# Row sums of a 64 MB array: from "112 rows and 16 behind" in one part to "127 rows and one behind" in four parts

## The chip, the core and the metric

The kernel runs on one core of a Trainium2 chip. A core has five instruction streams, of which three matter here: VectorE (DVE in the profile), ScalarE (ACT) and SyncE (SP), which does no arithmetic and issues DMA transfers. Sixteen DMA engines move data between the device memory (DRAM) and SBUF, the on-chip memory of 128 partitions. The metric is the device time of one launch in microseconds (us). Before the change it is 161.98 us, the median of three runs (161.95 to 162.12).

## The reference

```
batch, seq, dim = 32, 512, 1024          # x: float32, 64 MiB; multiplier = 0.5
out = (np.sum(x, axis=-1) * multiplier).astype(np.float32)
```

Seen flat, x has 16384 rows of 1024 floats (4 KB each), and every row becomes one number of `out`. Each byte of x is read once and used once: 67.11 MB go in and 65.5 KB come out.

## The kernel before

The 16384 rows are dealt to the 128 partitions, 128 rows each. Partition p owns 112 consecutive rows (`x_rows`), and, behind all of these, 16 further consecutive rows in the last 2048 rows of x (`x_last`). The output is cut the same way (`out_rows`, `out_last`). So every partition has 128 results, columns 0 to 127 of the SBUF tile `res`: columns 0 to 111 for its 112 rows, columns 112 to 127 for the last 16.

The work runs over eight blocks of 16 rows for each partition (8 MiB a block). The first seven are one load each (line 98), in which every partition gets one run of 64 KB. They go into a pool of three buffers, `x_pool`, so load b + 3 waits for the work on block b. The last block comes in five loads: 8, 5 and 2 rows (line 117), and then the last row in two pieces, of 544 and 480 floats (line 123), into the tile `end`. That is the sequence of blocks 16, 8, 5, 2, 1. SP issues all loads, in this order, on one queue, and the first three are moved ahead of the program's entry by `start_loads_at_entry`.

Six of the first seven blocks are summed by DVE with one instruction each (line 100, 16 rows), which is followed by a small scaling instruction (line 103). The seventh block is shared, half to DVE and eight rows to ACT (`act_row`, line 74). The last block's rows are shared row by row: ACT takes rows 4 to 7, 11, 12 and 14, and DVE the others with `dve_sum` (line 84), a fused add of two halves with an accumulator. The last row of each partition is summed by two such instructions, one for each piece: the first leaves its sum in `end` beside the second piece, and the second adds it in and writes column 127 of `res`.

There are two stores, both issued by SP. The early one (line 127) writes columns 0 to 111 when the first seven blocks are done, and stands in the queue behind the last loads. The last one (line 145) writes columns 112 to 127, 64 bytes for each partition, and waits for the last DVE instruction. In front of it stands an instruction that does nothing but wait for the loads and for ACT (`seen`, made by `nop_after`, line 63), so that these waits are over by then. Behind it another such instruction waits for the early store and the last DVE instruction; the program's end waits for the last store.

Of the kernel before, what the change touches and what calls it, by code (L numbers as in the profile page):

```python
# [1 line left out]

# [4 lines left out]


@with_exitstack
def kernel(  # L10
    ctx: ExitStack,
    tc: tile.TileContext,
    x: bass.AP,
    multiplier: float,
    out: bass.AP,
):

    nc = tc.nc
    P = nc.NUM_PARTITIONS
    fp32 = mybir.dt.float32  # L30
    ADD = mybir.AluOpType.add

    x_flat = x.flatten_outer_dims()
    N, D = x_flat.shape
    rows = N // P
    out_flat = out.rearrange("b s -> (b s)")
    mul = float(multiplier)

    B = 16
    n_blocks = rows // B  # L40
    assert N == P * rows and rows == n_blocks * B
    own = rows - B
    x_rows = x_flat[0 : P * own, :].rearrange("(p c) d -> p c d", p=P)
    x_last = x_flat[P * own : N, :].rearrange("(p c) d -> p c d", p=P)
    out_rows = out_flat[0 : P * own].rearrange("(p c) -> p c", p=P)
    out_last = out_flat[P * own : N].rearrange("(p c) -> p c", p=P)

    x_pool = ctx.enter_context(tc.tile_pool(name="x", bufs=3))
    res_pool = ctx.enter_context(tc.tile_pool(name="res", bufs=1))
    sums = res_pool.tile([P, rows], fp32, name="sums")  # L50
    res = res_pool.tile([P, rows], fp32, name="res")
    cut = 544
    at = 576
    end = res_pool.tile([P, at + D - cut], fp32, name="end")
    nc.vector.memset(end[:, at - 2 : at], 0.0)  # L55

    SYNC = mybir.DependencyInfo(mybir.DependencyClass.Sync, mybir.DependencyReason.DATA)
    ORDER = mybir.DependencyInfo(
        mybir.DependencyClass.NoSync, mybir.DependencyReason.SCHED_ONLY
    )  # L60

    def nop_after(engine, waits_for, follows):
        i = engine.nop()
        for w in waits_for:
            tc.add_manual_dep(i.ins, w.ins.name, SYNC, reason="end seen here")
        for f in follows:
            tc.add_manual_dep(i.ins, f.ins.name, ORDER, reason="in this order")
        return i

    loads = []  # L70
    acts = []

    def act_row(t, r, col):
        acts.append(nc.scalar.activation(  # L74
            out=t[:, r, :],
            in_=t[:, r, :],
            func=mybir.ActivationFunctionType.Copy,
            scale=mul,
            accum_out=res[:, col : col + 1],
        ))  # L80

    def dve_sum(row, dst, scale):
        mid = row.shape[-1] // 2
        return nc.vector.tensor_tensor_reduce(  # L84
            out=row[:, 0:mid],
            in0=row[:, 0:mid],
            in1=row[:, mid:],
            scale=scale,
            scalar=0.0,
            op0=ADD,  # L90
            op1=ADD,
            accum_out=dst,
        )

    for b in range(n_blocks - 1):
        c0 = b * B
        t = x_pool.tile([P, B, D], fp32, name="xb")
        loads.append(nc.sync.dma_start(out=t, in_=x_rows[:, c0 : c0 + B, :]))  # L98
        h = B if b < n_blocks - 2 else B // 2
        nc.vector.reduce_sum(  # L100
            out=sums[:, c0 : c0 + h], in_=t[:, 0:h, :], axis=mybir.AxisListType.X
        )
        nc.vector.tensor_single_scalar(  # L103
            out=res[:, c0 : c0 + h],
            in_=sums[:, c0 : c0 + h],
            scalar=mul,
            op=mybir.AluOpType.mult,
        )
        for r in range(h, B):
            act_row(t, r, c0 + r)  # L110

    c0 = (n_blocks - 1) * B
    t = x_pool.tile([P, B, D], fp32, name="xb")
    pieces = [(0, 8), (8, 13), (13, 15)]
    for lo, hi in pieces:
        loads.append(
            nc.sync.dma_start(  # L117
                out=t[:, lo:hi, :], in_=x_last[:, lo:hi, :]
            )
        )  # L120
    for to, lo, hi in ((0, 0, cut), (at, cut, D)):
        loads.append(
            nc.sync.dma_start(  # L123
                out=end[:, to : to + hi - lo], in_=x_last[:, B - 1, lo:hi]
            )
        )
    early = nc.sync.dma_start(out=out_rows, in_=res[:, 0:own])
    on_act = {4, 5, 6, 7, 11, 12, 14}
    for r in range(B - 1):
        if r in on_act:  # L130
            act_row(t, r, c0 + r)
        else:
            dve_sum(t[:, r, :], res[:, c0 + r : c0 + r + 1], mul)
    first = dve_sum(end[:, 0:cut], end[:, at - 1 : at], 1.0)
    part_seen = nop_after(nc.vector, [first], [])
    final = dve_sum(end[:, at - 2 :], res[:, rows - 1 : rows], mul)

    tc.add_manual_dep(final.ins, part_seen.ins.name, ORDER, reason="in this order")
    tc.declare_no_dep(final.ins, first.ins.name, reason="waited for by the nop in front")

    seen = nop_after(nc.sync, loads[-8:] + acts[-1:], [])
    store = nc.sync.dma_start(out=out_last, in_=res[:, own:])
    tc.add_manual_dep(store.ins, seen.ins.name, ORDER, reason="in this order")
    for a in acts[-len(on_act) :]:
        tc.declare_no_dep(store.ins, a.ins.name, reason="waited for by the nop in front")
    nop_after(nc.sync, [early, final], [store])

    def start_loads_at_entry(nc_):

        entry, *rest = nc_.main_func.blocks
        is_sp = lambda i: i.engine == mybir.EngineType.SP
        is_load = lambda i: type(i).__name__ == "InstDMACopy"
        for block in rest:
            body = list(block.instructions)
            own = [i for i in body if is_sp(i)]  # L160
            if not any(is_load(i) for i in own):
                continue
            lead = []
            for i in own:
                if not is_load(i) or i.sync_info.on_wait:
                    break
                lead.append(i)
            names = {i.name for i in lead}
            block.instructions = [i for i in body if i.name not in names]
            head = list(entry.instructions)  # L170
            at = next(
                k for k, i in enumerate(head) if is_sp(i) and type(i).__name__ == "InstDrain"
            )
            entry.instructions = head[:at] + lead + head[at:]
            return

    nc.at_finalize(start_loads_at_entry)


# [1 line left out]
_INS = ['x', 'multiplier']  # L181
_OUTS = [((32, 512), 'float32')]

_NUMBERS = {'multiplier': 0.5}


# [26 lines left out]
```

## Time and profile before

| what | value |
|---|---|
| median of three runs | 161.98 us (161.95 to 162.12) |
| profiled execution: span from first to last instruction | 160.2 us |
| median less that span (what lies around it) | 1.78 us |
| DVE busy | 119.3 us (74%), 35 instructions |
| ACT busy | 17.3 us (11%), 31 instructions |
| moved by DMA | 67.18 MB, 419 GB/s on average over the span |
| share of the 16 DMA engines' time in use | 97.6% |

The profile gives only the span of the profiled execution; its time outside is not recorded, so 1.78 us is taken from the median. "DMA share" is the mean busy share of the 16 DMA engines, and "us to landing" is the time from the start of a DMA's issue to the moment at which all of its data has arrived. "SPq" is SP issuing, as against computing.

### The profile page before, as it was taken

What the parts mean: (1) busy time and instruction counts of PE and PEld (TensorE: products, weight loads), DVE (VectorE), ACT (ScalarE), POOL (GpSimd) and SP (SyncE); (2) the same over time, 40 slices, a digit from 0 to 9 for tenths busy, and PEclk for the clock granted to TensorE, in tenths of its full rate; (3) what the DMA queues carried; (4) which work ended last, traced back from release to release, by engine and by line L of the source; (5) the groups of instructions that cost most, each with busy time, mean ns of one, the idle gap of its engine ahead of it and who ended that gap; (6) DMA issues with size and microseconds to landing.
All of it is one profiled execution on the core that took longest, in us unless ns stands there. A gap on an engine that the chain in (4) does not pass through costs nothing.

```text
span 160.2 us, 139 instructions
## 1 busy us (share of the span) xinstructions
DVE 119.3 (74%) x35; ACT 17.3 (11%) x31; POOL 0.2 (0%) x4
## 2 busy tenths in 40 slices
DVE  0000059998799968999599995999959999597543
ACT  0000000000000000000000000000000000599952
POOL 0000000000000000000000000000000000000000
DMA  8996996996996997997998989979969969999992
GB/s 278 507 524 262 524 524 262 524 524 262 524 507 278 524 475 311 524 442 344 524 425 360 524 360 425 524 327 458 524 295 491 524 278 507 393 401 422 424 395 76
DMA packets 2016, 67.18 MB, mean 419 GB/s; under 512 B 480, under 2 KB 608, under 8 KB 736
## 3 DMA queue, kind: packets, MB, share of 16 engines
q1 hardware_dynamic: 2016, 67.18, 97.6%
HBM read 67.11 MB, written 0.07 MB: 419 GB/s over the span
## 4 chain that ended last, share of the span: by engine, by line
DMA 75%; DVE 22%; SPq 1%; issue 0%; DVEq 0%
DMA xb<-in_x_dram 51%; DMA end<-in_x_dram 24%; DVE sums L100 22%; SPq L117 1%; SPq L123 0%; DVE end L84 0%; SPq L98 0%; DVE res L103 0%; DVEq L208 0%
## 5 line engine op out<-in xcount | busy, mean ns | idle before, releaser
L100 DVE TENSOR_REDUCE sums<-xb 128x16 f32<-128x16384 f32 (+1 forms) x7 | 112.0, 16002 | 31.5 <-DMA xb<-in_x_dram 31.5
L74 ACT ACT_TABLE_LOAD x1 | 1.3, 1283 | 138.0 <-DMA xb<-in_x_dram 138.0
L74 ACT ACTIVATE xb<-xb 128x1024 f32<-128x1024 f32 x15 | 15.7, 1044 | 2.1 <-DMA xb<-in_x_dram 2.1
L84 DVE CUSTOM_DVE_ANT_0 xb<-xb 128x512 f32<-128x512 f32 x8 | 5.1, 690 | 4.9 <-DMA xb<-in_x_dram 4.9
L74 ACT ACTIVATION_READ_ACCUMULATOR xb<-xb 128x1 f32 x15 | 2.8, 187 | 0.0
L55 DVE MEMSET end<- 128x2 f32 x1 | 0.1, 60 | 1.8 <-PEq L194 1.8
L103 DVE TENSOR_SCALAR res<-sums 128x16 f32<-128x16 f32 (+1 forms) x7 | 1.2, 174 | 0.2
L84 DVE CUSTOM_DVE_ANT_0 end<-end 128x272 f32<-128x272 f32 (+1 forms) x2 | 0.9, 426 | 0.2 <-DMA end<-in_x_dram 0.2
L84 DVE DVE_READ_ACCUMULATOR2_ANT res<- 128x1 f32 x9 | 0.7, 83 | 0.0
L194 POOL MEMSET const-bfloat16-1.0<- 128x1 bf16 x1 | 0.1, 102 | 0.0
L194 POOL MEMSET const-uint8-127<- 128x1 uint8 x1 | 0.1, 102 | 0.0
L194 POOL MEMSET const-float32-0.0<- 128x1 f32 x1 | 0.1, 99 | 0.2 <-issue 0.2
L194 POOL MEMSET const-float32-1.0<- 128x1 f32 x1 | 0.1, 99 | 0.0
L84 DVE DVE_READ_ACCUMULATOR2_ANT end<- 128x1 f32 x1 | 0.1, 83 | 0.0
## 6 DMA issues: line engine op xcount, KB each, us to landing
xb<-in_x_dram SPq DMA_DIRECT2D x1, 4096.0 KB, 31.1
xb<-in_x_dram SPq DMA_DIRECT2D x1, 2560.0 KB, 36.9
xb<-in_x_dram SPq DMA_DIRECT2D x1, 1024.0 KB, 38.9
end<-in_x_dram SPq DMA_DIRECT2D x1, 272.0 KB, 39.0
end<-in_x_dram SPq DMA_DIRECT2D x1, 240.0 KB, 39.2
xb<-in_x_dram SPq DMA_DIRECT2D x7, 40.8
out_dram<-res SPq DMA_DIRECT2D x1, 56.0 KB, 10.0
out_dram<-res SPq DMA_DIRECT2D x1, 8.0 KB, 1.4
```

What stands on the lines that cost most here:

```text
L55: nc.vector.memset(end[:, at - 2 : at], 0.0)
L74: acts.append(nc.scalar.activation(out=t[:, r, :], in_=t[:, r, :], func=mybir.ActivationFunctionType.Copy, scale=mul, accum_out=res[:, col ...
L84: return nc.vector.tensor_tensor_reduce(out=row[:, 0:mid], in0=row[:, 0:mid], in1=row[:, mid:], scale=scale, scalar=0.0, op0=ADD, op1=ADD, ...
L100: nc.vector.reduce_sum(out=sums[:, c0 : c0 + h], in_=t[:, 0:h, :], axis=mybir.AxisListType.X)
L103: nc.vector.tensor_single_scalar(out=res[:, c0 : c0 + h], in_=sums[:, c0 : c0 + h], scalar=mul, op=mybir.AluOpType.mult,)
L117: nc.sync.dma_start(out=t[:, lo:hi, :], in_=x_last[:, lo:hi, :])
L194: nc = _bacc.Bacc("TRN2", target_bir_lowering=False, num_devices=1)
```

## The change

Rows are dealt in another way, and there are three stores in place of two.

- x is seen as four parts of 4096 rows. Partition p = 4g + b (g from 0 to 31, b from 0 to 3) owns, in part b, the 127 rows from row 127g on, and one single row from the part's last 32 rows, row 4064 + g. `x_rows`, `x_single`, `out_rows` and `out_single` say this, with the DRAM side in three dimensions: 32 (g), 4 (b), and a run.
- The loads have the same sizes and order as before. Blocks 0 to 6 and the pieces of 8, 5 and 2 rows are now from the 127 consecutive rows. The last row, in two pieces, is the single one.
- The early store still writes columns 0 to 111, now as 128 runs of 448 bytes that begin 508 bytes apart in each part; before, these runs joined to one contiguous range.
- A new store, `second`, is issued by ACT behind its last row. It writes columns 112 to 126: 128 runs of 60 bytes.
- The last store, on SP, writes column 127 alone: 4 bytes for each partition, which in `out` form four contiguous runs of 128 bytes, one at the end of each part.
- The waiting instruction at the end waits for `second` too.

```diff
+    G = P // 4
+    long = rows - 1
+    x_regions = x_flat.rearrange("(b n) d -> b n d", b=4)
+    out_regions = out_flat.rearrange("(b n) -> b n", b=4)
+    x_rows = x_regions[:, 0 : G * long, :].rearrange("b (g c) d -> g b c d", c=long)
+    x_single = x_regions[:, G * long :, :].rearrange("b g d -> g b d")
+    out_rows = out_regions[:, 0 : G * long].rearrange("b (g c) -> g b c", c=long)
+    out_single = out_regions[:, G * long :].rearrange("b (g o) -> g b o", o=1)
...
-        loads.append(nc.sync.dma_start(out=t, in_=x_rows[:, c0 : c0 + B, :]))
+        loads.append(nc.sync.dma_start(out=t, in_=x_rows[:, :, c0 : c0 + B, :]))
...
-                out=t[:, lo:hi, :], in_=x_last[:, lo:hi, :]
+                out=t[:, lo:hi, :], in_=x_rows[:, :, own + lo : own + hi, :]
...
-                out=end[:, to : to + hi - lo], in_=x_last[:, B - 1, lo:hi]
+                out=end[:, to : to + hi - lo], in_=x_single[:, :, lo:hi]
...
-    early = nc.sync.dma_start(out=out_rows, in_=res[:, 0:own])
+    early = nc.sync.dma_start(out=out_rows[:, :, 0:own], in_=res[:, 0:own])
...
+    second = nc.scalar.dma_start(out=out_rows[:, :, own:], in_=res[:, own:long])
     seen = nop_after(nc.sync, loads[-8:] + acts[-1:], [])
-    store = nc.sync.dma_start(out=out_last, in_=res[:, own:])
+    store = nc.sync.dma_start(out=out_single, in_=res[:, long:])
...
-    nop_after(nc.sync, [early, final], [store])
+    nop_after(nc.sync, [early, second, final], [store])
```

More of the change, by code (lines that the diff above doesn't have):

```diff
@@ L42 @@
     own = rows - B
[L43 to L46, printed above, removed]
+    G = P // 4
[6 more added lines that the diff above has]
+    out_single = out_regions[:, G * long :].rearrange("b (g o) -> g b o", o=1)
     x_pool = ctx.enter_context(tc.tile_pool(name="x", bufs=3))
```

## The prediction

> **What bounds the kernel now.** I read the chain that ended last first, to see what the end hangs on. Its columns are start, length and what.
>
> ```profile
> 99.28 17.23 DVE sums L100
> 116.52 0.02 issue
> 116.54 0.19 DVE res L103
> ...
> 117.91 0.43 SPq L123
> 118.34 0.04 issue
> 118.38 39.17 DMA end<-in_x_dram
> 157.55 0.02 issue
> 157.58 0.41 DVE end L84
> ```
>
> The chain alternates between loads and DVE's sums only because a load's issue waits for a free buffer. The last step shows the truth: the last load was issued at 118.38 and landed 39.17 us later, because it stood behind what was already queued. So the second view is the busy table by stretches: length, busy time of DVE, ACT and POOL, clock, DMA share, GB/s.
>
> ```profile
> 5.00:22.00 17.00, 0.09 (x1) 0.00 (x0) 0.00 (x0) 1.00 1.00 432
> 41.20:60.60 19.40, 17.41 (x3) 0.00 (x0) 0.00 (x0) 1.00 1.00 432
> ...
> 138.00:147.70 9.70, 8.85 (x3) 9.64 (x17) 0.00 (x0) 1.00 0.99 425
> ...
> 153.80:156.30 2.50, 1.94 (x7) 2.20 (x5) 0.00 (x0) 1.00 0.98 399
> 156.30:157.60 1.30, 1.14 (x5) 1.14 (x2) 0.00 (x0) 1.00 0.56 197
> 157.60:160.20 2.60, 0.39 (x2) 0.00 (x0) 0.00 (x0) 1.00 0.04 3
> ```
>
> All sixteen DMA engines are busy all the time from 5 us on, at 432 GB/s, and DVE needs 17.4 us of each 19.4 us block. The packet records agree: one 64 KB run takes 2.418 us on its engine, 27.1 GB/s, and 16 x 27.1 = 434 GB/s. The load stream is the bound until 157.1, when the last engine is through; the first is through at 156.6. What comes behind it is a fixed tail, shown by the timeline (start, length) and the list of DMA issues (KB, us to landing).
>
> ```profile
> 157.58 0.41 DVE L84 CUSTOM_DVE_ANT_0 end<-end 128x241 f32<-128x241 f32 x1 [0.16 <-DMA end<-in_x_dram]
> 157.91 0.08 DVE L84 DVE_READ_ACCUMULATOR2_ANT res<- 128x1 f32 x1
> 158.02 0.34 SPq L145 DMA_DIRECT2D out_dram<-res  x1
> ```
>
> ```profile
> out_dram<-res SPq DMA_DIRECT2D x1, 56.0 KB, 10.0
> out_dram<-res SPq DMA_DIRECT2D x1, 8.0 KB, 1.4
> ```
>
> The last store is issued at 158.02 and has landed at 159.45 (1.43 us by the records); 0.75 us of closing barriers make 160.20. The early store (56 KB) was issued at 147.79 and landed 10.0 us later, at 157.79: it waits in the queue behind the loads. The sum below is made against this execution: span 160.20, and 1.78 us around it to the median of 161.98.
>
> **The change, part by part.**
>
> *Loads: the same bytes, sizes, order and number.* Only the DRAM addresses move. A partition's runs began 112 rows (448 KB) apart; now four neighbouring partitions read 16 MB apart, and every fourth is 127 rows (508 KB) further. Runs stay contiguous, 64 KB in the seven large blocks. Since an engine is at 2.418 us for such a run through the whole stream, there is nothing to gain there. The one slow place is the start: the first run of each engine took 3.07 to 3.47 us (one 2.77), about 0.8 us over 2.418. I read that as the first access's latency and take 0; lower bound -0.8. Upwards the trace shows no other address pattern, so there is no row: 1% of the stream's 156 us would cost 1.6 us, and a pattern that halved the rate 156 us. I take 0, because the reads stay long contiguous runs like those of the rows above, and the last pieces, only 2 KB long and 64 KB apart, still went at 24.7 GB/s on an engine (88 ns for 2176 bytes), so this stream has borne a change of steps before.
>
> The Trainium skill, "DMA: Bandwidth & Descriptors", section "Latency and other measured facts", has a rule against this: partition rows a large power of two apart slow DMA copies to less than half (103 against 214 GB/s at 4 and 8 MiB), and a pad of 4 KiB mends it. By it the loads would cost up to some 160 us more, an estimate, if streams 16 MiB apart ran side by side; 508 KiB, being 512 less 4, is on its good side. No run here shows it yet.
>
> *Issue of the loads, with a three-dimensional DRAM side.* Issues took 0.38 us (the first) to 0.46 us. Eleven of the twelve lie beside queued transfers (39 us deep at the end); if that cover were gone they would cost their 0.4 us each. The first is exposed. Bounds 0 and +0.08 (0.46 - 0.38); I take +0.05.
>
> *DVE and ACT sums:* the same instructions in the same order, 0.
>
> *Early store:* 448-byte runs 508 bytes apart instead of joined. It used to land at 157.79, and nothing that mattered waited for it. Now something does: in the changed program ACT's new store carries a wait for the early store's landing, since their ranges of `out` interleave. I keep 157.79; the bound is that its runs take twice as long (they ran from 156.42 to 157.28 by the records), so landing up to 0.9 us later.
>
> *Second store, on ACT.* It waits for DVE's last row but the single one (column 125, written by 156.99), for ACT's own last row (column 126, 157.44), and for the early store, 157.79, which is the last. Issue 157.85, and with SP's 1.43 us to landing it is in at 159.28, beside the last store's 159.45: hidden by 0.17 us. Nothing is queued behind it on ACT but the end barrier. If the early store or the issue on ACT takes over 0.17 us more, it sets the end. ACT issues no DMA in the trace of before. Bounds from SP's rows: nothing, to a full landing behind the store, +1.43. I take +0.10, for two issues that overlap from 158.02 to 158.20 and for twice the small writes landing together (their runs occupy 0.2 us, 158.86 to 159.07, per store).
>
> *Last store: 128 runs of 4 bytes instead of 64.* The number of runs stays, and that governs: a 64-byte run takes 8 to 11 ns, a 4-byte completion record 9 ns. So the bytes save nothing; at best the 0.2 us in which the runs pass (-0.2). Against it, 32 pieces from different engines now fall into one 128-byte range. Each run's completion came 0.36 to 0.39 us after it; if an engine's eight pieces went strictly one after the other, that is 8 x 0.36 = 2.9 us, the upper bound. I take +0.15, near the lower end, since the other small stores landed at the common pace. Its issue has three dimensions: 0.34 us up to 0.46; I take +0.05. The wait for ACT's rows goes from its conditions, but it had long been over (157.44), so 0.
>
> *Closing:* one wait more on SP, before the landing of the last store. It is hidden while `second` lands first; otherwise two waits of some 0.06 us follow it. I take +0.05.
>
> Sum: 0.05 + 0.10 + 0.15 + 0.05 + 0.05 = +0.40. The span becomes 160.6, the time 162.4 us. A measurement of this kernel can tell about 0.2% (0.32 us) from no change, so this is slower by a little.
>
> **The rivals.**
>
> *The tail stays hidden (no change), 162.0.* For it: `second` has 0.17 us of cover, a store of fewer bytes may land as early, issues differ by less than 0.1. Then every term is near zero: 161.7 to 162.3. Against it: the new wait for the early store leaves little room.
>
> *The start gets faster (faster), 161.5.* One mechanism: the 0.8 us that the first runs of the engines took too long is due to the addresses, and the new ones avoid most of it; the whole stream and with it the tail move forward. It decides once it saves over 0.7 us with the tail's +0.4, or over 0.32 us with a tail at 0. Price: -0.4 to -0.8, 161.2 to 161.6. Against it: a slow first access is what any stream that starts cold would show, and later 64 KB runs show no trace of address trouble.
>
> *The load stream gets slower, 163 to over 300.* The sixteen engines run at an even 27.1 GB/s each, which holds only while neither DRAM nor the split of 128 partitions over engines makes two engines meet. The change touches both: the DRAM side has 32 as its outer dimension, the SBUF side 128. It shows from 0.2% of the rate on (+0.3); 1% gives 163.6, half the rate some 318 us. Against it: the number of engines and the runs are unchanged.
>
> **How the numbers follow.** Tail longer, as summed: 0.40 (162.3 to 163.4). No change: 0.25. Start faster: 0.17. Stream slower: 0.18, of which 0.08 below 164 and 0.10 beyond. So faster 0.17, same 0.25, slower 0.58. The range leaves out the stream's large losses (0.10) and the lowest part of the faster case: 161.5 to 164.0, which holds the no-change case and most of the price of `second` (+1.43). The likeliest case's own range is 162.3 to 163.4.
>
> **What would show it.** In the changed profile: 64 KB loads still 19.4 us apart and a DMA share of 1.00 near 432 GB/s (else the stream rival); the first DVE sum still at 21.9 (earlier: the start rival); the last DVE instruction near 157.6; a DMA issue on ACT near 157.85 and one on SP near 158.02; landings of 1.4 to 1.6 us for both, and SP's last wait for out_dram a few tenths over 1.0 us. If ACT's issue comes clearly later than 157.9, or its landing ends last by more than half a microsecond, the second store was undersized. Anything over 164 means the stream was misjudged, and the tail's account is then of no weight.

## The result and the profile after

The changed kernel takes 169.79 us (median of four runs, 169.61 to 170.41) against 162.0 us before. The ratio is 1.0489, with a 95% interval of 1.0471 to 1.0508: slower by 7.8 us. The profiled execution took 169.61 us, of which 167.8 us are its span; 1.8 us lie around it as before.

The load stream is as it was. In the busy table by stretches (length, DVE, ACT, POOL, clock, DMA share, GB/s) of the changed kernel:

```profile
5.00:22.00 17.00, 0.00 (x0) 0.00 (x0) 0.00 (x0) 1.00 1.00 432
...
41.20:60.60 19.40, 17.39 (x2) 0.00 (x0) 0.00 (x0) 1.00 1.01 436
...
157.00:163.00 6.00, 1.55 (x6) 1.36 (x4) 0.00 (x0) 1.00 0.12 31
163.00:165.00 2.00, 0.00 (x0) 0.00 (x0) 0.00 (x0) 1.00 0.00 0
165.00:168.00 3.00, 0.00 (x0) 0.00 (x0) 0.00 (x0) 1.00 0.00 0
```

The engines still move 432 to 436 GB/s without a gap. The time is lost at the two ends. First the start, in the chain that ended last (start, length, what):

```profile
0.00 0.66 SPq L102
0.66 0.05 issue
0.70 41.73 DMA xb<-in_x_dram
42.44 0.02 issue
42.46 17.23 DVE sums L104
```

Before the change the same chain had:

```profile
0.00 0.38 SPq L98
...
41.23 17.23 DVE sums L100
```

The first issue takes 0.66 us instead of 0.38, and DVE's second sum begins at 42.46 instead of 41.23, 1.23 us later. This shift stays to the end of the loads: DVE's last sum begins at 158.84 instead of 157.58, 1.26 us later. Now the tail, in the timeline (start, length), the list of DMA issues (KB, us to landing) and the waits of SP (us, times, longest):

```profile
158.84 0.41 DVE L88 CUSTOM_DVE_ANT_0 end<-end 128x241 f32<-128x241 f32 x1 [0.19 <-DMA end<-in_x_dram]
159.16 0.63 ACTq L148 DMA_DIRECT2D out_dram<-res  x1
159.18 0.08 DVE L88 DVE_READ_ACCUMULATOR2_ANT res<- 128x1 f32 x1
159.29 0.57 SPq L150 DMA_DIRECT2D out_dram<-res  x1
```

```profile
out_dram<-res SPq DMA_DIRECT2D x1, 56.0 KB, 10.0
out_dram<-res ACTq DMA_DIRECT2D x1, 7.5 KB, 1.9
out_dram<-res SPq DMA_DIRECT2D x1, 0.5 KB, 7.8
```

```profile
SPq L213 <- DMA out_dram<-res: 6.0, 1, 6.0
```

Before the change this last wait of SP was:

```profile
SPq L208 <- DMA out_dram<-res: 1.0, 1, 1.0
```

The last store now moves 0.5 KB instead of 8 KB and needs 7.79 us from its issue to landing instead of 1.43, so 6.36 us more. The records of single pieces show that all 128 pieces had left the engines at 160.92; the sixteen engines' completions then trickle in from 161.92 to 167.07, where before they came within 0.17 us. With 1.26 us from the start this is 7.62 us, and the spans differ by 7.6.

So two questions had to be settled by experiments: what makes the last store land so late, and what delays the start. For the store there were three theories. Crowding: pieces that fall close together in DRAM hold one another up. Size: any 4-byte write is slow. Neighbours: the pieces collide with those of the other two stores. For the start there were two: the third dimension of the loads, or their new addresses.

### The profile page after: what moved, and what is told of

It reads as the page before. It is cut to its first block, busy times and chain, and to the rows that moved or that the text cites. A ratio compares the mean times of both kernels' runs of the same rounds, so it can differ in the third digit from the quotient of the medians.

```text
span 167.8 us, 141 instructions
## 1 busy us (share of the span) xinstructions
DVE 119.3 (71%) x35; ACT 17.3 (10%) x31; POOL 0.2 (0%) x4
## 4 chain that ended last, share of the span: by engine, by line
DMA 72%; DVE 21%; SPq 2%; issue 0%; DVEq 0%
DMA xb<-in_x_dram 49%; DMA end<-in_x_dram 23%; DVE sums L104 21%; SPq L121 1%; SPq L102 0%; SPq L127 0%; DVE end L88 0%; DVE res L107 0%; DVEq L213 0%
```

## The experiments

### One part instead of four

The changed kernel with 127 rows and one behind in a single part. The DRAM sides have two dimensions again; column 127 is 512 contiguous bytes, still written in 4-byte pieces.

```diff
-    x_rows = x_regions[:, 0 : G * long, :].rearrange("b (g c) d -> g b c d", c=long)
-    x_single = x_regions[:, G * long :, :].rearrange("b g d -> g b d")
+    x_rows = x_flat[0 : P * long, :].rearrange("(p c) d -> p c d", c=long)
+    x_single = x_flat[P * long :, :]
...
-    out_single = out_regions[:, G * long :].rearrange("b (g o) -> g b o", o=1)
+    out_single = out_flat[P * long :].rearrange("(p o) -> p o", o=1)
...
```

> The changed kernel in one part instead of four: 128 partitions own 127 consecutive rows and one of the last 128 rows, so the DRAM side of every transfer has two dimensions again, and the last column is 512 contiguous bytes of out, written in 4-byte pieces. The theory for the 1.2 us at the start (a third dimension makes issue and hand-out to the DMA engines slower): first load lands at 21.9 us as before the change, issues 0.38 to 0.46 us. Its rival (the new addresses are slower to read at first): 508 KB steps remain, so up to 1.2 us may remain if these are the cause, nothing if the 16 MB steps are. For the 6.4 us at the end, the theory of crowding (4-byte writes into the same few DRAM lines are done one after another) and that of size (any 4-byte write to DRAM is slow) both expect a landing of 6 to 8 us after the issue, so about 168.4 us in all; the theory of neighbours (writes beside the other two stores collide) expects the same or less.

Measured: 167.82 us, ratio 1.0355 (1.0339 to 1.0371). The chain's beginning and the list of DMA issues:

```profile
0.00 0.37 SPq L100
0.37 0.05 issue
0.42 40.80 DMA xb<-in_x_dram
```

```profile
out_dram<-res ACTq DMA_DIRECT2D x1, 7.5 KB, 1.5
out_dram<-res SPq DMA_DIRECT2D x1, 0.5 KB, 7.0
```

The start of this execution is the old one (issue 0.37 us, first load at 21.91). That steps of 127 rows cost nothing in two dimensions is not shown by it: the seven further kernels below with the same large loads had their first load at 21.96 to 22.31, and the one profile of the kernel before at 21.89, so a few tenths of a microsecond may be theirs. The late landing stays, at 7.0 us. Third dimension and four parts are not its cause.

### Four parts, with 16 rows behind

The kernel before in four parts, its last store of 64 bytes for each partition kept.

```diff
-    x_rows = x_flat[0 : P * own, :].rearrange("(p c) d -> p c d", p=P)
-    x_last = x_flat[P * own : N, :].rearrange("(p c) d -> p c d", p=P)
...
+    x_rows = x_regions[:, 0 : G * own, :].rearrange("b (g c) d -> g b c d", c=own)
+    x_last = x_regions[:, G * own :, :].rearrange("b (g c) d -> g b c d", c=B)
...
```

> The kernel before, in four parts: in each, 32 partitions own 112 consecutive rows and 16 behind them; two stores, the last of 64 bytes for each partition. Three-dimensional theory for the start: first load lands 1.2 us later than before the change, at 23.1, and the last store's issue takes 0.57 us instead of 0.34. Crowding and size both expect the last landing back at about 1.4 + 0.4 us, so 161.98 + 1.2 + 0.4 = 163.6 us in all. If the tail were the fault of three dimensions, it would stay near 169.

Measured: 163.14 us, ratio 1.007 (1.0055 to 1.0085). The first load lands at 22.55, less late than expected, and the last store 1.81 us after its issue. Four parts with their third dimension, in loads and stores, cost about 1.2 us, and the rest of the 7.8 us goes with the one-column store.

### The third dimension alone

The kernel before; only the seven large loads get a third dimension, at nearly the old addresses.

```diff
-    x_rows = x_flat[0 : P * own, :].rearrange("(p c) d -> p c d", p=P)
+    G = P // 4
+    x_groups = x_flat[0 : G * (4 * own + 1), :].rearrange("(g r) d -> g r d", g=G)
+    x_rows = x_groups[:, 0 : 4 * own, :].rearrange("g (b c) d -> g b c d", c=own)
...
```

> The kernel before, whose seven large loads alone get a third dimension on the DRAM side: groups of four partitions, each group moved by one row against the last, so addresses move by at most 31 rows (the sums are of these rows, so part of the output belongs to rows displaced by up to 31). Stores and last block as before. If three dimensions make the start slow: first load lands at 23.1, all else as before, 163.2 us. If the addresses 16 MB apart do: lands at 21.9, 162.0 us.

Measured: 162.57 us, ratio 1.0036 (1.0022 to 1.005), between the two expectations. The beginning of its chain:

```profile
0.00 0.63 SPq L100
0.63 0.06 issue
0.69 41.05 DMA xb<-in_x_dram
```

The issue takes 0.63 us with a third dimension at nearly the old addresses, and the first load lands at 22.42, 0.53 us late. The piece records show how: the first engine begins at 1.42 instead of 1.01, and the last of the sixteen at 2.24 instead of 1.51. This is not one execution's chance: over all profiles of this case the last engine begins between 1.35 and 2.05 in the ten kernels with two-dimensional large loads, and between 2.13 and 2.52 in the eight with three. So half of the 1.2 us is explained. The other half was still open.

### The last store alone, as in the change

The changed kernel without its other two stores.

```diff
-    early = nc.sync.dma_start(out=out_rows[:, :, 0:own], in_=res[:, 0:own])
...
-    second = nc.scalar.dma_start(out=out_rows[:, :, own:], in_=res[:, own:long])
...
-    nop_after(nc.sync, [early, second, final], [store])
+    nop_after(nc.sync, [final], [store])
```

> The changed kernel without its early and second stores: only column 127 is written, the rest of out is left out. Crowding and size: the last store still lands 7.8 us after its issue, 169.5 us in all. Neighbours: 1.9 us after its issue, some 163.6 us in all.

Measured: 169.08 us in one run, landing 7.0 us after the issue:

```profile
out_dram<-res SPq DMA_DIRECT2D x1, 0.5 KB, 7.0
```

The theory of neighbours falls: the store lands late with no other store in the program. (The 0.8 us between 7.79 and 7.0 are one execution each, and stay open.)

### The pieces' distance

Crowding and size were still to be told apart. In the one-part kernel, with the last store alone, the 4-byte pieces were put 4, 8, 16, 64 and 512 bytes apart, from the start of `out` on. (At 4 bytes this changes only the place in `out`, and the landing stays: 7.14 us against the one-part kernel's 6.99.) The edit, for 16 bytes:

```diff
-    out_single = out_flat[P * long :].rearrange("(p o) -> p o", o=1)
+    step = 4
+    out_single = out_flat[0 : P * step].rearrange("(p o) -> p o", o=step)[:, 0:1]
```

> The one-part kernel with 127 rows and one behind, without its early and second stores: the only store writes 4 bytes for each partition, at the start of out, 4 bytes apart (512 contiguous bytes; the rest of out is left out). Crowding and size both expect what the one-part kernel showed: landing 7.0 us after the issue, some 167.8 us in all.

> As the store alone at 4 bytes apart, but 16 bytes apart, so that a quarter as many writes share any stretch of out (only these numbers are written). Crowding: the part of the landing over 1.4 us falls from 5.6 to about a quarter, landing 2.5 to 3.5 us. Size: 7 us still.

> As the store alone, 64 bytes apart (only these numbers are written). Crowding with a stretch of 64 bytes: landing 1.4 to 1.6 us, 162.0 us in all; with a larger stretch, more. Size: 7 us still.

> As the store alone, 512 bytes apart (only these numbers are written). Crowding: landing 1.4 to 1.6 us, 162.0 us in all. Size: 7 us still, 167.6 us in all.

> The store alone of the one-part kernel, 8 bytes apart (only these numbers are written). At 16 bytes it landed in 1.44 us, at 4 bytes in 7.1 us. If writes collide when they share 16 bytes: two do so now, and the landing lies between, some 3 us or more. If they collide only where they share 8 bytes or adjoin: 1.44 us.

Measured, one run each:

| pieces of 4 bytes, bytes apart | pieces in 16 bytes | landing after issue | device time |
|---|---|---|---|
| 4 | 4 | 7.14 us | 168.01 us |
| 8 | 2 | 2.94 us | 163.88 us |
| 16 | 1 | 1.44 us | 162.63 us |
| 64 | 1 | 1.45 us | 162.29 us |
| 512 | 1 | 1.44 us | 162.28 us |

The lists of DMA issues at 4, 8 and 16 bytes, in this order:

```profile
out_dram<-res SPq DMA_DIRECT2D x1, 0.5 KB, 7.1
```

```profile
out_dram<-res SPq DMA_DIRECT2D x1, 0.5 KB, 2.9
```

```profile
out_dram<-res SPq DMA_DIRECT2D x1, 0.5 KB, 1.4
```

The same 128 pieces of 4 bytes, 512 bytes in all, land in 1.44 us or in 7.14 us: size is not the cause, closeness is. My expectation for 16 bytes (2.5 to 3.5 us) missed. The loss doesn't fall in proportion to the distance; it ends sharply between 8 and 16 bytes. (The kernel at 16 bytes is 0.3 us slower than those at 64 and 512 with the same landing: its first load landed 0.14 to 0.16 us later than theirs, at 22.31, and the last load 0.36 to 0.37 us later. That part of the time is the load stream's.)

### The pieces' width

If what counts is that two pieces share 16 bytes, adjoining pieces of 8 bytes must collide and adjoining ones of 16 bytes must not. The last two, or four, columns were stored alone, side by side.

```diff
-    step = 1
-    out_single = out_flat[0 : P * step].rearrange("(p o) -> p o", o=step)[:, 0:1]
+    wide = 4
+    out_single = out_flat[0 : P * wide].rearrange("(p o) -> p o", o=wide)
...
-    store = nc.sync.dma_start(out=out_single, in_=res[:, long:])
+    store = nc.sync.dma_start(out=out_single, in_=res[:, rows - wide :])
```

> The store alone of the one-part kernel, but of the last two columns, 8 adjoining bytes for each partition, 1 KB in all (the rest of out is left out). Stretch of 16 bytes shared by two pieces: as with 4 bytes at steps of 8, about 2.9 us to landing. If the size of a piece, 4 bytes, is what hurts when neighbours are near: 1.4 us.

> The store alone of the one-part kernel, of the last four columns, 16 adjoining bytes for each partition, 2 KB in all (the rest of out is left out). Stretch of 16 bytes: no piece shares one, 1.4 us to landing. A larger stretch, or any adjoining pieces: over 2 us.

The lists of DMA issues, of 8 and of 16 bytes:

```profile
out_dram<-res SPq DMA_DIRECT2D x1, 1.0 KB, 2.7
```

```profile
out_dram<-res SPq DMA_DIRECT2D x1, 2.0 KB, 1.4
```

Landing 2.68 us and 1.45 us; 163.62 and 162.10 us. Two pieces of 8 bytes in one stretch of 16 collide about as two of 4 bytes do, and pieces of 16 bytes side by side don't. So what these runs show is a stretch of 16 bytes that several pieces share. Every one of these stores began at the start of `out`; whether the stretches lie at multiples of 16 bytes or any two pieces less than 16 bytes apart collide was not tried.

### Where the rest of the start comes from

The kernel before, stores and last block unchanged, its large loads in three dimensions from three more sets of addresses. The edit for the changed kernel's own addresses:

```diff
-    x_rows = x_flat[0 : P * own, :].rearrange("(p c) d -> p c d", p=P)
+    G = P // 4
+    x_regions = x_flat.rearrange("(b n) d -> b n d", b=4)
+    x_rows = x_regions[:, 0 : G * 127, :].rearrange("b (g c) d -> g b c d", c=127)
...
```

> The kernel before, stores and last block unchanged, with only the seven large loads taken from the addresses of the changed kernel (four parts, runs 127 rows apart, of which the first 112 rows are used, so the sums belong to other rows). If the 1.2 us at the start of the changed kernel come from its loads alone: first load lands at 23.1, 163.2 us. If half of it came from the rest of the program: 22.4 to 22.5 and 162.6 us.

> The kernel before, stores and last block unchanged, the seven large loads in three dimensions but with neighbouring partitions 127 rows apart in one stretch (groups of four, moved by one row each; sums of displaced rows). If the 0.6 us beyond the cost of the third dimension come from the step of 127 rows: first load at 23.1, 163.2 us; if from the 16 MB between the parts: 22.4, 162.6 us.

> As the one with four parts and 127 rows, but runs 112 rows apart (sums of displaced rows). If the 0.6 us come from the 16 MB between the parts alone: first load at 23.1, 163.2 us; the four-part kernel with 16 rows behind suggests 22.5 and 162.6 us, so that it takes both the parts and the step of 127 rows.

| large loads in three dimensions | first load lands | median | ratio to before, with interval |
|---|---|---|---|
| near, 112 rows apart | 22.42 | 162.57 | 1.0036 (1.0022 to 1.005) |
| near, 127 rows apart | 22.39 | 162.62 | 1.0042 (1.0029 to 1.0054) |
| four parts, 112 rows apart | 22.68 | 162.80 | 1.0051 (1.0036 to 1.0066) |
| four parts, 127 rows apart | 22.70 | 162.95 | 1.0057 (1.0042 to 1.0072) |

In three dimensions the step of 127 rows instead of 112 does nothing that can be told. Going from near to four parts moves the first load by 0.3 us in the profiles, and the medians by 0.2 to 0.3 us, but the intervals overlap. With the very addresses of the change the cost is 0.98 us (162.95 less 161.97), neither of the two expectations. What makes it up to the 1.2 us of the changed kernel is open, but the records show where it lies. In all 18 profiles of this case the first load lands 17.2 to 17.4 us after the last engine has ended its first 64 KB piece; in the changed kernel that end is at 5.85, in the kernel before at 4.62, which makes the whole shift. It depends on when an engine starts and on how long its first piece takes (2.4 to 4.0 us in the records, with two dimensions as with three), so it changes from execution to execution: the landing varied by 0.4 us (21.91 to 22.31) between the two-dimensional one-part kernels above, whose large loads are the same.

### The changed kernel without the collision

As the last store alone in four parts, with the pieces 16 bytes apart. They now lie in one stretch at the start of `out` instead of in four.

```diff
-    out_single = out_regions[:, G * long :].rearrange("b (g o) -> g b o", o=1)
+    out_spread = out_flat[0 : 4 * P].rearrange("(b g o) -> b g o", b=4, o=4)
+    out_single = out_spread[:, :, 0:1].rearrange("b g o -> g b o")
```

> The changed kernel's loads and last store in three dimensions, without its early and second stores, and with the 4-byte pieces of column 127 put 16 bytes apart (only these numbers are written). If the whole loss of the change is crowding in the last store plus the start: last landing 1.8 us after the issue instead of 7.0, first load at 22.7 to 23.1, 163.1 to 163.5 us in all, less by 5.6 us than the same kernel with the pieces adjoining. If crowding counts only with two-dimensional stores: more.

Measured: 163.49 us, ratio 1.009 (1.0076 to 1.0104); landing 1.86 us after the issue, first load at 22.83:

```profile
out_dram<-res SPq DMA_DIRECT2D x1, 0.5 KB, 1.9
```

Against the 169.08 us of the same kernel with adjoining pieces, 5.6 us are gone, 5.1 of them in the landing (7.00 to 1.86); in the profiles the last load, too, landed 0.6 us earlier. The remaining 1.5 us are the start (about 1.0 us) and a last store in three dimensions (1.86 instead of 1.43 us).

### A repair: 124 rows and 4 behind

The one-part kernel with four rows of each partition behind.

```diff
-    long = rows - 1
+    behind = 4
+    long = rows - behind
...
-    pieces = [(0, 8), (8, 13), (13, 15)]
+    pieces = [(0, 8), (8, 12), (12, 13), (13, 15)]
...
```

> A repair in one part: 124 consecutive rows and 4 behind, so that the last store writes 16 adjoining bytes for each partition (2 KB in all) and a second store from ACT writes the 12 columns before; the last block comes as 8, 4, 1, 2 and 1 rows. If pieces that fill their 16 bytes do not collide: last landing 1.4 us after the issue, 161.9 to 162.2 us, no gain on the kernel before, since its 64-byte store already lands in 1.43 us. If adjoining pieces collide in larger stretches: 163 us or more.

Measured: 162.69 us, ratio 1.0039 (1.0024 to 1.0055). The last store does land 1.41 us after its issue. The mend works and gains nothing; it is 0.7 us slower than the kernel before. In its timeline the rows before the last arrive late:

```profile
154.62 1.06 ACT L77 ACTIVATE xb<-xb 128x1024 f32<-128x1024 f32 x1 [0.48 <-DMA xb<-in_x_dram]
...
155.01 0.37 ACTq L151 DMA_DIRECT2D out_dram<-res  x1
...
157.16 1.06 ACT L77 ACTIVATE xb<-xb 128x1024 f32<-128x1024 f32 x1 [1.39 <-DMA xb<-in_x_dram]
```

The kernel before had the last of these rows earlier:

```profile
156.29 1.06 ACT L74 ACTIVATE xb<-xb 128x1024 f32<-128x1024 f32 x1 [0.30 <-DMA xb<-in_x_dram]
```

The two rows before the last are there at 157.16 instead of 156.29. In this execution 0.35 us of that came with the first load. The eight rows of the last block's first load landed 0.40 us late (148.06 against 147.67), and the row that is now a load of its own, the thirteenth, 0.83 us late (154.60 against 153.77). The second store was issued only after that, at 155.01, and the two rows that follow are 0.88 us late, hardly more. So the extra load costs about 0.4 us in this execution, and the second store hardly anything that shows. The 4 KB pieces of the extra load took 0.16 to 0.34 us each on their engines.

## Why the prediction was wrong

The direction was right and the size was not: +0.4 us forecast, +7.8 measured, outside the range.

*The step that failed: "Last store: 128 runs of 4 bytes instead of 64".* I took +0.15 us and held 2.9 us to be the upper bound, from eight pieces of one engine, each with its own 0.36 us to completion. Measured are +6.36 us. About 5.1 of them are the crowding: so much goes, in the kernel with this store alone, when the pieces are put 16 bytes apart at the start of `out` (7.00 to 1.86), and the place in `out` made no such difference (7.14 against 6.99 in one part). Some 0.4 are the third dimension of the store (1.86 against 1.43), for which I took +0.05, and 0.8 (7.79 against 7.00) stay open. The part of the step that was right: the pieces pass the engines as fast as before, by number and not by bytes, and had left them at 160.92. I named the crowding (32 pieces in 128 bytes) and then chose a value "near the lower end, since the other small stores landed at the common pace". That was the mistake of reading: those stores were 64 and 448 bytes wide, so no row of the profile had two pieces in one stretch of 16 bytes. The nearest row was not near in what mattered, and the bound counted one engine's pieces only.

*The second failure: "Issue of the loads", +0.05 us with a bound of 0.08.* The bound came from the spread among two-dimensional issues. I also read two rows wrongly: the issues before took 0.33 to 0.46 us, not from 0.38 on, and the engines' first pieces 2.95 to 3.47 us besides the one of 2.77, not from 3.07 on. The first issue took 0.66 us instead of 0.38, and what followed was larger: the engines were handed their first pieces between 1.43 and 2.52 instead of 1.01 and 1.51. The step is worth +1.2 us, and since the stream is full behind it, all of it reaches the end. The experiment with the third dimension alone gives 0.6 us of it, the four parts some 0.2 to 0.3; the rest is open.

*Early store and second store on ACT:* the waits were as worked out. The early store landed at 159.06, which is 157.79 and the shift; ACT's store waited for exactly this, was issued at 159.16 (predicted 157.85, and the shift), and landed 1.87 us later instead of 1.43. That is 0.44 more, over the 0.17 us of cover that I had given it: beside a last store that landed in 1.43 us it would have set the end. It is in at 161.02, six microseconds before the last store, so its +0.10 and the closing wait cost nothing here.

*Loads, nothing:* right. 19.4 us a block, 432 GB/s. The Trainium skill's "DMA: Bandwidth & Descriptors", section "Latency and other measured facts", with its rule on rows a large power of two apart, didn't bear on this stream: with parts 16 MB apart it ran at its old rate of 432 GB/s. That is no test of the rule, which is on one equal step from each partition's row to the next.

The rivals: the start moved, but to the slow side; the stream kept its rate; the tail was not hidden, since nothing stands behind the last store. The range reached to 164.0 for the sake of the stream and the second store. The case that came true, the crowded last store, was on the list, with too low a ceiling, and had no chance of its own. The sign "anything over 164 means the stream was misjudged" pointed the wrong way: the time is 169.79 with an unchanged stream. Of the 0.40 us that I added up, 0.25 stood on the terms that did grow (the loads' issue, the last store and its issue), so the direction is not mere luck; the 0.15 for the second store and the closing measured nothing.

## What to carry to other kernels

A last store that writes one 4-byte result for each partition to adjoining addresses is a trap: let each piece fill the 16 bytes it lies in, even if more columns have to wait for the last one; 64 bytes for each partition landed as fast (1.43 us) as 4 bytes 16 apart (1.44 us). Whatever delays the first transfer of a kernel whose DMA engines never pause is paid in full at the end, so give the first load the simplest pattern: with two dimensions on the DRAM side the last engine started at 1.35 to 2.05 us, with three at 2.13 to 2.52. And where a bound rests on the nearest row, say in what the row is near; here the number of pieces was the same, and what counted was how close together they lie.

## What the runs showed of the hardware that I had not expected

- 4-byte or 8-byte pieces that share 16 bytes of DRAM land late: 2.7 to 2.9 us with two in a stretch, 7.0 to 7.8 us with four, against 1.4 us with one. With 128 pieces in all, four in a stretch instead of two cost about four times the delay (5.7 us over the 1.44, against 1.5). Why was not tried.
- In the timelines a third dimension on the DRAM side costs SP 0.53 to 0.67 us for each issue instead of 0.33 to 0.48, and ACT 0.63 instead of 0.37.
- A store's engines can be long done (160.92) while its landing is still 6 us away (167.07): the DMA share of 0.00 from 163 us on, with SP waiting for `out_dram`, is how that looks in a profile.
- The Trainium skill, "DMA: Bandwidth & Descriptors", section "Specifications", puts the limit for transfers at line rate at 512 bytes and says that smaller ones are read, modified and written. In these runs stores in pieces of 4, 16 and 64 bytes, all below it, landed within 0.05 us of each other as long as no two shared 16 bytes; that is their landing, and no run here measured their rate.
